# Two parts of the matmul array as neighbours: reordering the small products of an RWKV mixer

## The chip, the cores and the metric

The kernel runs on one core of a Trainium2 chip. That core has five engines with a queue each: TensorE (PE in the profile; its weight loads are PEld), VectorE (DVE), ScalarE (ACT), GpSimd (POOL) and SyncE (SP), which issues transfers here. Each engine takes its own instructions in order, and engines wait for each other through semaphores. Matmuls write to PSUM, which has eight banks; a tile of the kernel with 512 f32 columns fills one.

The metric is device time in microseconds: the median of several executions of the kernel, as they were shown.

## The reference

The reference is a two-layer encoder trunk with 1024 positions of width 1024. Layer 0 mixes with two head groups side by side: RWKV-7 (8 heads of 64) and gated DeltaNet (4 heads of 128). Layer 1 mixes with chunked attention. Each layer then has a squared-ReLU MLP and a gated per-layer embedding. Only the RWKV group, and an inverse that both groups use, are touched:

```python
def rwkv7_group(...):
    ...
    w_log = -jax.nn.softplus(-(w0 + jnp.tanh(xw @ w1) @ w2)) - 0.5
    decay = jnp.exp(-jnp.exp(w_log))
    a = jax.nn.sigmoid(a0 + (xa @ a1) @ a2)
    ...
    y = wkv7_scan(rh, heads(decay), kh, vh, -kk, kk * ah)
    ...

def step(state, inp):                       # of wkv7_scan
    r_t, w_t, k_t, v_t, a_t, b_t = inp
    sa = jnp.einsum('bhij,bhj->bhi', state, a_t)
    state = state * w_t[:, :, None, :] + sa[..., None] * b_t[:, :, None, :] + v_t[..., None] * k_t[:, :, None, :]
    return state, jnp.einsum('bhij,bhj->bhi', state, r_t)
```

The kernel does not step through positions. It works in chunks of 128 positions: within a chunk the recurrence is a unit lower triangular system, whose matrix is N, and whose inverse is formed once for each chunk and head. The state is carried from chunk to chunk.

## The kernel before

**Units and lanes.** Layer 0's mixer is cut into 16 units: for each half of the sequence (512 positions, four chunks of 128), four RWKV pairs of heads and four DeltaNet heads, alternating. A unit goes through five lanes, each a Python generator: `in` (projections), `front` (decay, N and its scores, the start of the inverse), `mid` (the end of the inverse), `back` (the recurrence over four chunks) and `post` (group norm and gate). `run` (L123) plays the lanes against a clock of its own: each matmul adds a modelled time to `self.now` (`mm`, L151), and each `yield` of a name holds a lane back for the time that the table `LAT` has for it, while other lanes go on. This sets the program order. When the context is closed, a scheduler that simulates the program (L1950) may still move an instruction ahead of others that are not ready. The projections are dense 128 x 128 x 512 products (tile `dps`) in a two-pass type (hi and lo parts); they fill the time in which other lanes wait.

**Banks.** Two of the eight PSUM banks hold the dense products. Six have one tag each: `tp` (front), `iz` (inverse), `pm` (masked scores), `ch` (steps of the recurrence), `y` (its output) and `pp` (post lane, `post_bank`, L520).

**An f32 product** appears in the trace as two passes, each a weight load and a matmul, so counts of the profile are twice the number of products. A shape such as 64*128 in a row of PE is the part of the array: 64 rows (the contraction) by 128 columns (the output's partitions).

**Low-rank products** (`rwkv_front`, L758). `lwa` holds, in partitions 0 to 63, the decay's low-rank input and, in 64 to 127, that of a. psw (L781) multiplies the upper half with `wa2`, psa (L807) the lower half; both go through `ptile`, bank `tp`, and both are read by a tanh on ACT (L783 and L809). Between them lies the work on the decay and a pause, `rwkv_front0` (L804).

**N scores** (L833 to L840). For each head h of the pair, rows 64h to 64h + 63: four 64 x 128 x 128 products, one for each chunk, into one bank `tp`; then four scaled evacuations on ACT into N; then a pause, `rwkv_front3`. So head 1 starts after head 0's pause.

**The inverse** (`inverse_end`, L393). N's diagonal blocks of 16 are inverted on POOL beforehand; then blocks are joined to 32, 64 and 128 for N = 8 (RWKV: four chunks of two heads) or 4 (DeltaNet: four chunks) matrices at once. Steps 0 and 1 join to 32, with products that go round all four 32-row groups. Steps 2 and 3 (tiles `T32`, `Z`, `X32`) join to 64: for each of two blocks, i = 0 and i = 2, all N products of 32 x 32 x 32 follow each other, first those of i = 0. Steps 5 and 6 (tile `TZ`, L455 and L460) join to 128: N products of 64 x 64 x 64 follow each other in one part of the array, their results lie in one half of the partitions, and one ACT copy takes them out.

**The recurrence** (`rwkv_back`, L871), for each of four chunks c: pw (inverse's right side), a copy W on ACT, pu = X W, scaled to U on DVE, then pu2, the state update, with one 128 x 64 x 64 product of Ktm and Vt and one of Btm and U for each head; S2 on DVE; the scores of the next chunk; and y: one 128 x 128 x 128 product of the state Sf with AR, and for each head one of Vt and one of U with masked scores `pmq`, which land in that head's half of the partitions. pw reads `pmq` of both heads.

Of the kernel before, what the change touches and what calls it, by code (L numbers as in the profile page):

```python
# [11 lines left out]
AF = mybir.ActivationFunctionType  # L12
# [5 lines left out]
P = 128  # L18
# [5 lines left out]
C = 128  # L24
# [80 lines left out]
class Trunk:  # L105
# [45 lines left out]
    def mm(self, out, lhsT, rhs, start, stop):  # L151
        n, m = 1, 1
        for c in rhs.shape[1:]:
            n *= c
        for c in lhsT.shape[1:]:
            m *= c
        if rhs.dtype == F32:
            self.now += 2 * max(n / 1200, m * 0.0007)
        else:
            self.now += max(n / 2400, m * 0.00035)  # L160
        return self.nc.tensor.matmul(out, lhsT, rhs, start=start, stop=stop)  # L161

    def tr(self, out, in_, ident):
        self.now += 0.107
# [228 lines left out]
    def inverse_end(self, Xp, B, N, F):  # L393

        nc, h2 = self.nc, self.mid
        V, A, G = nc.vector, nc.scalar, nc.gpsimd
        cur, curT = Xp[:, :, 0:16], Xp[:, :, 16:32]
        m1, m2 = self.half[:, 0:1], self.half[:, 1:2]
        quad = [slice(32 * i, 32 * i + 32) for i in range(4)]
        up, lo = slice(0, 64), slice(64, 128)  # L400

        def bank(w):
            return self.psm.tile([P, N, w], F32, tag="iz", name="iz")

# [24 lines left out]
        Z = T2  # L429
        for i in (0, 2):  # L430
            for g in range(N):
                self.mm(pz[quad[i + 1], g, :], B[quad[i], g, quad[i + 1]], T2[quad[i], g, :], start=True, stop=True)
        for i, cp in ((0, A.copy), (2, V.tensor_copy)):
            cp(Z[quad[i + 1]], pz[quad[i + 1]])
        for i in range(4):
            G.tensor_copy(F[quad[i], :, quad[i]], X2[quad[i]])
        yield f"inverse{N}_2"
        px = bank(32)
        for i in (0, 2):
            for g in range(N):  # L440
                self.mm(px[quad[i], g, :], Z[quad[i + 1], g, :], X2[quad[i + 1], g, :], start=True, stop=True)
        for i, cp in ((0, A.copy), (2, V.tensor_copy)):
            cp(F[quad[i], :, quad[i + 1]], px[quad[i]])
        yield f"inverse{N}_3"

        pt = bank(64)
# [7 lines left out]
        for g in range(N):  # L454
            self.mm(pz[lo, g, :], B[up, g, lo], TZ[up, g, :], start=True, stop=True)  # L455
        A.copy(TZ[lo], pz[lo])
        yield f"inverse{N}_5"
        px = bank(64)
        for g in range(N):
            self.mm(px[up, g, :], TZ[lo, g, :], F[lo, g, lo], start=True, stop=True)  # L460
        A.copy(F[up, :, lo], px[up])
        yield f"inverse{N}_6"


# [293 lines left out]
    def rwkv_front(self, p, hf, sc, raws, u):  # L758
        nc, h2, fr, sm, psm = self.nc, self.h2, self.fr, self.sm, self.psm
        V, A, G = nc.vector, nc.scalar, nc.gpsimd  # L760
        t2 = self.t2
# [9 lines left out]
        def ptile():  # L771
            return psm.tile([P, HB], F32, tag="tp", name="tp")
# [4 lines left out]
        sq = t2()  # L777
        A.activation(sq, kkr, AF.Square)

        psw = ptile()  # L780
        self.mm(psw, self.wa2[0:64, p * P:(p + 1) * P], sc["lwa"][0:64], start=True, stop=True)  # L781
        lw = t2()
        A.activation(lw, psw, AF.Tanh, bias=self.dv["hw0"][:, p:p + 1], scale=0.5)  # L783
        V.tensor_scalar(lw, lw, -0.5 * EXPM05, -0.5 * EXPM05, op0=ALU.mult, op1=ALU.add)
# [16 lines left out]
        A.activation(E, L, AF.Exp)  # L801
        Em = t2([P, 4, C])
        A.activation(Em, L[:, :, 1:C + 1], AF.Exp, scale=-1.0)
        yield "rwkv_front0"  # L804

        psa = ptile()
        self.mm(psa, self.wa2[64:128, p * P:(p + 1) * P], sc["lwa"][64:128], start=True, stop=True)  # L807
        ta = t2()
        A.activation(ta, psa, AF.Tanh, bias=self.dv["ha0"][:, p:p + 1], scale=0.5)  # L809
        yield "rwkv_front1"  # L810
        pst = ptile()
        for c in range(4):
# [1 line left out]
        cc = sm.tile([P, 8], F32, tag="cc", name="cc", bufs=4)  # L814
# [9 lines left out]
        Bt, Kt = t2(tag="b"), t2(tag="b")  # L824
# [5 lines left out]
            yield ("mid", u - 2)  # L830

        N = self.mid.tile([P, 8, P], F32, tag="n8", name="N")
        for h in range(2):  # L833
            sl = slice(64 * h, 64 * h + 64)
            ps = ptile()
            for c in range(4):
                self.mm(ps[:, c * C:(c + 1) * C], Bt[sl, c * C:(c + 1) * C], AR[sl, c, 0, :], start=True, stop=True)
            for c in range(4):
                A.activation(N[:, 4 * h + c, :], ps[:, c * C:(c + 1) * C], AF.Copy, scale=cc[:, 2 * c + h:2 * c + h + 1])
# [31 lines left out]
    def rwkv_back(self, p, hf, sc, st, u):  # L871
# [35 lines left out]
        for c in range(4):  # L907
# [36 lines left out]
            for h in range(2):  # L944
# [1009 lines left out]
```

## Time and profile before

| | |
|---|---|
| median of three runs | 3194.34 us (3192.11 to 3196.0) |
| the profiled execution | 3200.01 us, span 3198.3 us |
| mean granted clock of TensorE | 0.974 |
| PE in 0 to 110 us | 91.33 us busy |
| PE in 945 to 970 us (the last head of layer 0) | 18.76 us busy |
| PE in 970 to 1750 us (layer 0's MLP and what follows) | 780.00 us busy |
| PE in 1750 to 2395 us (layer 1's attention) | 590.80 us busy |
| PE in 2395 to 3198.3 us (layer 1's MLP and what follows) | 798.18 us busy |

The profile is of one execution. A row of its groups names the line, the engine, the operation and the tiles (out<-in), the part of the array, the shape and the count, then busy time, the mean of one, and the idle time ahead of it. As every matmul is recorded by one helper, they all have line L161 (transposes L165) and are told apart by their tiles: `tp<-lao,wa` are the low-rank products, `tp<-AR,b` the N scores, `iz<-T,N`, `iz<-X,T`, `iz<-TZ,N` and `iz<-F,TZ` the inverse (with Ng in place of N for DeltaNet), `ch<-b,tm` and `ch<-U,tm` the state update, `py<-...` the output y. A row of the timeline begins with the start and the length in us and ends with the count of passes in it. Matmuls are pipelined, so lengths overlap.

### The profile page before, as it was taken

To read this page: it belongs to the slowest core of one execution; us is meant where nothing else is said; L and a number is where in the kernel's file an instruction comes from. 1 tells how busy PE (TensorE), PEld (TensorE's weight loads), DVE (VectorE), ACT (ScalarE), POOL (GpSimd) and SP (SyncE) were. 2 spreads that over 40 slices of the span, in tenths; PEclk is the share of its full clock that TensorE was granted. 3 is DMA by queue.
4 is the path that set the end of the run, shared out by engine and by line. 5 is a ranking of instruction groups with operands and counts; after the bars stand their busy time and mean duration, and the time that the engine had idled before them with its cause. 6 is when DMAs were issued, how large, how long until landed. Compare 5 with 4: busy or idle time off the path is not lost.

```text
span 3198.3 us, 46044 instructions
## 1 busy us (share of the span) xinstructions
PE 3102.1 (97%) x17576; PEld 2565.6 (80%) x17576; DVE 2013.2 (63%) x4020; ACT 1384.2 (43%) x2608; POOL 531.5 (17%) x978
## 2 busy tenths in 40 slices
PE   7999999999999999999999898999899999999999
PEld 5777777777777888888888888988778888888887
DVE  6566675556748666655546576776768666655552
ACT  4333333334326555322123477777756555312121
POOL 6334442433410000000004211010110000000002
PEclk8999899999899999999999999999999999999999
DMA  3322112212325433523213210110156433522213
GB/s 120 94 63 60 47 46 67 70 61 70 129 95 194 155 119 108 192 93 106 92 51 128 70 36 32 45 41 16 69 177 209 150 121 109 185 105 92 106 47 105
DMA packets 144716, 309.60 MB, mean 97 GB/s; under 512 B 40944, under 2 KB 43120, under 8 KB 144496
## 3 DMA queue, kind: packets, MB, share of 16 engines
q1 hardware_dynamic: 126064, 273.10, 25.6%
q10 hardware_dynamic: 18432, 33.56, 2.7%
q8 instruction: 138, 2.26, 0.3%
q14 instruction: 82, 0.67, 0.1%
HBM read 232.16 MB, written 74.45 MB: 96 GB/s over the span
## 4 chain that ended last, share of the span: by engine, by line
PE 85%; DVE 7%; ACT 3%; DMA 2%; issue 1%; POOL 0%; SPq 0%; ACTq 0%; DVEq 0%; POOLq 0%
PE dps L161 70%; PE ch L161 3%; PE iz L161 2%; PE pm L161 2%; PE tp L161 1%; PE po L161 1%; PE py L161 1%; DVE ptile L318 1%; PE pt L165 1%; DMA wraw<-in_w_qkv 1%; PE sn L161 1%; PE pp L161 1%; DVE pb L1795 1%; PE sc L161 1%; ACT pb L1808 1%
## 5 line engine op out<-in xcount | busy, mean ns | idle before, releaser
L161 PE MATMUL dps<-r,act 128*128 128x512 f32 x3528 | 824.4, 392 | 0.0
L161 PEld LDWEIGHTS dps<-r,act 128*128 128x128 f32 x3528 | 662.1, 188 | 145.7
L161 PE MATMUL dps<-xg,whi 128*128 128x512 f32 x1280 | 438.2, 418 | 11.7 <-ACT xg L320 7.3
L161 PE MATMUL dps<-late,act 128*128 128x512 f32 x1536 | 352.9, 391 | 0.0
L161 PEld LDWEIGHTS dps<-late,act 128*128 128x128 f32 x1536 | 288.4, 188 | 63.1
L161 PE MATMUL dps<-wq,act 128*128 128x384 f32 x1536 | 304.8, 344 | 5.8 <-DVE vs L1704 3.1
L1452 POOL TENSOR_TENSOR pn<-pn,prs 128x512 f32<-128x512 f32 x32 | 45.5, 1426 | 1590.7 <-ACT prs L354 1496.3
L161 PEld LDWEIGHTS dps<-xg,whi 128*128 128x128 f32 x1280 | 248.4, 199 | 75.2 <-issue 10.7
L161 PEld LDWEIGHTS dps<-wq,act 128*128 128x128 f32 x1536 | 265.6, 191 | 10.4 <-DVE vs L1704 5.1
L161 PE MATMUL dps<-xg,wlo 128*128 128x512 f32 x640 | 266.4, 416 | 3.1 <-DVE wlo L277 3.1
L1328 DVE TENSOR_TENSOR late<-late,dps 128x512 f32<-128x512 f32 x224 | 152.9, 685 | 150.1 <-PE dps L161 119.2
L1427 DVE TENSOR_TENSOR xw<-xw,dps 128x512 f32<-128x512 f32 x192 | 131.5, 685 | 148.4 <-PE dps L161 145.5
L1226 ACT CAST act<-act 128x1024 fp32r<-128x1024 f32 (+1 forms) x99 | 94.8, 964 | 285.2 <-DMA act<-in_w 124.2
L1226 ACT CAST act<-late 128x512 fp32r<-128x512 f32 x210 | 124.5, 618 | 135.9 <-PE dps L161 117.0
L1227 DVE TENSOR_TENSOR act<-late,act 128x512 fp32r<-128x512 f32 x210 | 139.9, 687 | 26.1 <-ACT act L1226 25.9
L161 PEld LDWEIGHTS dps<-xg,wlo 128*128 128x128 f32 x640 | 126.9, 198 | 34.1 <-issue 4.8
L161 PE MATMUL dps<-xw,act 128*128 128x512 f32 x576 | 138.9, 392 | 0.0
L276 ACT CAST whi<-wraw 128x1024 fp32r<-128x1024 f32 x78 | 81.7, 1047 | 124.2 <-PE dps L161 74.4
L161 PEld LDWEIGHTS dps<-xw,act 128*128 128x128 f32 x576 | 108.1, 188 | 24.1
L1227 DVE TENSOR_TENSOR act<-act 128x1024 fp32r<-128x1024 f32 (+1 forms) x99 | 109.9, 1115 | 21.0 <-ACT act L1226 19.8
L161 PE MATMUL po<-ptile,vs 128*128 128x256 f32 (+1 forms) x576 | 104.9, 297 | 17.1 <-DVE ptile L318 7.7
L277 DVE TENSOR_TENSOR wlo<-wraw,whi 128x1024 fp32r<-128x1024 f32 x78 | 101.4, 1301 | 25.6 <-ACT whi L276 25.6
(472 smaller groups left out, 5369.4 us busy)
## 6 DMA issues: line engine op xcount, KB each, us to landing
act<-in_w SPq DMA_DIRECT2D x68, 512.0 KB
hd<-late ACTq DMA_DIRECT2D x128, 256.0 KB
late<-in_w SPq DMA_DIRECT2D x60, 512.0 KB
wraw<-in_w_in SPq DMA_DIRECT2D x56, 512.0 KB
act<-hd SPq DMA_DIRECT2D x56, 512.0 KB
wraw<-in_w_out SPq DMA_DIRECT2D x21, 512.0 KB
wraw<-in_w_qkv SPq DMA_DIRECT2D x21, 512.0 KB
pn<-pnd SPq DMA_DIRECT2D x32, 256.0 KB
```

Of the source, the lines that this page charges most:

```text
L161: return self.nc.tensor.matmul(out, lhsT, rhs, start=start, stop=stop)
L165: return self.nc.tensor.transpose(out, in_, ident)
L276: nc.scalar.copy(hi, raw)
L277: nc.vector.tensor_tensor(lo, raw, hi.bitcast(F32), op=ALU.subtract)
L318: nc.vector.tensor_tensor(dst[:, 1, sl], src, dst[:, 0, sl].bitcast(F32), op=ALU.subtract)
L1226: A.copy(hi, s)
L1227: V.tensor_tensor(lo, s, hi.bitcast(F32), op=ALU.subtract)
L1328: V.tensor_tensor(r, t, u, op=ALU.add)
L1427: V.tensor_tensor(x[n][:, sl], x[n][:, sl], ps, op=ALU.add)
L1452: G.tensor_tensor(pn, pn, prs[:, sl], op=ALU.mult)
L1795: V.tensor_tensor_reduce(S, pn[:, 0:nn * P], toep[:, (3 - nn) * P:], op0=ALU.add, op1=ALU.max, scale=1.0, scalar=NEG, accum_out=mx[:, 0:1])
L1808: A.activation(S, S, AF.Exp, bias=mx[:, 2:3], accum_out=l[:, 0:1])
```

## The change

- A helper, `together`, adds edges without semaphores between the matmuls of a list, so that they keep that order.
- psw and psa are issued as neighbours, psa first, psa into the post lane's bank `pp`. Both tanh follow, that of psa first. The pause `rwkv_front0` goes.
- The N scores of the two heads alternate, chunk by chunk, into two banks (`tp` for head 0, `pp` for head 1); all eight evacuations follow, those of head 1 first. One pause `rwkv_front3` is left of two.
- In steps 2 and 3 of the inverse the loops over i and g are exchanged, so that products in different parts of the array alternate.
- In steps 5 and 6 the results of even g go to the upper half of the partitions and those of odd g to the lower; two ACT copies take them out.
- In the recurrence, the state's product for y is issued ahead of the pause `rwkv_back5`; the state update goes Ktm of both heads, then Btm of both heads; and the head products of y follow it in the same manner, Vt of both heads, then U of both heads, ahead of S2 and of the next scores.

The table `LAT` and the modelled times of `mm` are as before.

```diff
+    def together(self, products):
+
+        edge = mybir.DependencyInfo(mybir.DependencyClass.NoSync, mybir.DependencyReason.DATA)
+        for u, v in zip(products, products[1:]):
+            self.tc.add_manual_dep(v.ins, u.ins.name, edge, reason="together")
...
-        for i in (0, 2):
-            for g in range(N):
+        for g in range(N):
+            for i in (0, 2):
                 self.mm(pz[quad[i + 1], g, :], B[quad[i], g, quad[i + 1]], T2[quad[i], g, :], start=True, stop=True)
...
+        part = lambda t, e: t[:, e::2, :]
+
+        def both(ps, f):
+            for g in range(N):
+                f(ps[up if g % 2 == 0 else lo, g, :], g)
+
+        def out(dst, ps):
+            for e, r in ((0, up), (1, lo)):
+                A.copy(part(dst, e), part(ps[r], e))
...
-        for g in range(N):
-            self.mm(pz[lo, g, :], B[up, g, lo], TZ[up, g, :], start=True, stop=True)
-        A.copy(TZ[lo], pz[lo])
+        both(pz, lambda o, g: self.mm(o, B[up, g, lo], TZ[up, g, :], start=True, stop=True))
+        out(TZ[lo], pz)
...
-        psw = ptile()
-        self.mm(psw, self.wa2[0:64, p * P:(p + 1) * P], sc["lwa"][0:64], start=True, stop=True)
+        psw, psa = ptile(), self.post_bank()
+        self.together([self.mm(ps, self.wa2[r, p * P:(p + 1) * P], sc["lwa"][r], start=True, stop=True)
+                       for ps, r in ((psa, slice(64, 128)), (psw, slice(0, 64)))])
+
+        ta = t2()
+        A.activation(ta, psa, AF.Tanh, bias=self.dv["ha0"][:, p:p + 1], scale=0.5)
...
-        yield "rwkv_front0"
-
-        psa = ptile()
-        self.mm(psa, self.wa2[64:128, p * P:(p + 1) * P], sc["lwa"][64:128], start=True, stop=True)
-        ta = t2()
-        A.activation(ta, psa, AF.Tanh, bias=self.dv["ha0"][:, p:p + 1], scale=0.5)
         yield "rwkv_front1"
...
+        pn = [ptile(), self.post_bank()]
+        ms = []
+        for c in range(4):
+            for h in (1, 0):
+                sl = slice(64 * h, 64 * h + 64)
+                ms.append(self.mm(pn[h][:, c * C:(c + 1) * C], Bt[sl, c * C:(c + 1) * C], AR[sl, c, 0, :],
+                                  start=True, stop=True))
+        self.together(ms)
+        for h in (1, 0):
             for c in range(4):
-                self.mm(ps[:, c * C:(c + 1) * C], Bt[sl, c * C:(c + 1) * C], AR[sl, c, 0, :], start=True, stop=True)
-            for c in range(4):
-                A.activation(N[:, 4 * h + c, :], ps[:, c * C:(c + 1) * C], AF.Copy, scale=cc[:, 2 * c + h:2 * c + h + 1])
-            yield "rwkv_front3"
+                A.activation(N[:, 4 * h + c, :], pn[h][:, c * C:(c + 1) * C], AF.Copy, scale=cc[:, 2 * c + h:2 * c + h + 1])
+        yield "rwkv_front3"
...
+            py_c = py[:, c * C:(c + 1) * C]
+            self.mm(py_c, Sf, AR[:, c, 1, :], start=True, stop=False)
             yield "rwkv_back5"
+
             pu2 = psm.tile([P, HB], F32, tag="ch", name="ch")
-            for h in range(2):
-                self.mm(pu2[hs[h], 0:64], Ktm[:, c, hs[h]], Vt[:, c, hs[h]], start=True, stop=False)
-                self.mm(pu2[hs[h], 0:64], Btm[:, c, hs[h]], U[:, hs[h]], start=False, stop=True)
+            for t, v in ((Ktm, Vt[:, c]), (Btm, U)):
+                for h in range(2):
+                    self.mm(pu2[hs[h], 0:64], t[:, c, hs[h]], v[:, hs[h]], start=t is Ktm, stop=t is Btm)
+            for v, j in ((Vt[:, c], 2), (U, 0)):
+                for h in range(2):
+                    self.mm(py_c[hs[h]], v[:, hs[h]], pmq[c, h][:, j, :], start=False, stop=j == 0)
...
-            py_c = py[:, c * C:(c + 1) * C]
-            self.mm(py_c, Sf, AR[:, c, 1, :], start=True, stop=False)
-            for h in range(2):
-                self.mm(py_c[hs[h]], Vt[:, c, hs[h]], pmq[c, h][:, 2, :], start=False, stop=False)
-                self.mm(py_c[hs[h]], U[:, hs[h]], pmq[c, h][:, 0, :], start=False, stop=True)
             yield "rwkv_back6"
```

More of the change, by code (lines that the diff above doesn't have):

```diff
@@ L438, in inverse_end @@
         px = bank(32)
-        for i in (0, 2):
-            for g in range(N):
+        for g in range(N):
+            for i in (0, 2):
                 self.mm(px[quad[i], g, :], Z[quad[i + 1], g, :], X2[quad[i + 1], g, :], start=True, stop=True)
@@ L444, in inverse_end @@
         yield f"inverse{N}_3"
+        part = lambda t, e: t[:, e::2, :]
+        def both(ps, f):
+            for g in range(N):
+                f(ps[up if g % 2 == 0 else lo, g, :], g)
+        def out(dst, ps):
+            for e, r in ((0, up), (1, lo)):
+                A.copy(part(dst, e), part(ps[r], e))
         pt = bank(64)
@@ L453, in inverse_end @@
         pz = bank(64)
-        for g in range(N):
-            self.mm(pz[lo, g, :], B[up, g, lo], TZ[up, g, :], start=True, stop=True)
-        A.copy(TZ[lo], pz[lo])
+        both(pz, lambda o, g: self.mm(o, B[up, g, lo], TZ[up, g, :], start=True, stop=True))
+        out(TZ[lo], pz)
         yield f"inverse{N}_5"
         px = bank(64)
-        for g in range(N):
-            self.mm(px[up, g, :], TZ[lo, g, :], F[lo, g, lo], start=True, stop=True)
-        A.copy(F[up, :, lo], px[up])
+        both(px, lambda o, g: self.mm(o, TZ[lo, g, :], F[lo, g, lo], start=True, stop=True))
+        out(F[up, :, lo], px)
         yield f"inverse{N}_6"
@@ L832, in rwkv_front @@
         N = self.mid.tile([P, 8, P], F32, tag="n8", name="N")
-        for h in range(2):
-            sl = slice(64 * h, 64 * h + 64)
-            ps = ptile()
+        pn = [ptile(), self.post_bank()]
[7 more added lines that the diff above has]
+        for h in (1, 0):
             for c in range(4):
-                self.mm(ps[:, c * C:(c + 1) * C], Bt[sl, c * C:(c + 1) * C], AR[sl, c, 0, :], start=True, stop=True)
-            for c in range(4):
-                A.activation(N[:, 4 * h + c, :], ps[:, c * C:(c + 1) * C], AF.Copy, scale=cc[:, 2 * c + h:2 * c + h + 1])
-            yield "rwkv_front3"
+                A.activation(N[:, 4 * h + c, :], pn[h][:, c * C:(c + 1) * C], AF.Copy, scale=cc[:, 2 * c + h:2 * c + h + 1])
+        yield "rwkv_front3"
         X = self.inverse_start(N, 8)
@@ L941, in rwkv_back @@
                 scores(c + 1, 1)
-            py_c = py[:, c * C:(c + 1) * C]
-            self.mm(py_c, Sf, AR[:, c, 1, :], start=True, stop=False)
-            for h in range(2):
-                self.mm(py_c[hs[h]], Vt[:, c, hs[h]], pmq[c, h][:, 2, :], start=False, stop=False)
-                self.mm(py_c[hs[h]], U[:, hs[h]], pmq[c, h][:, 0, :], start=False, stop=True)
             yield "rwkv_back6"
```

## The prediction

> **What bounds the kernel now.** I read four views in this order: the page, a table by stretches, the waits of the matmul engine, and then its timeline around each product that the diff moves. First the page:
>
> ```profile
> span 3198.3 us, 46044 instructions
> ...
> PE 3102.1 (97%) x17576; PEld 2565.6 (80%) x17576; DVE 2013.2 (63%) x4020; ACT 1384.2 (43%) x2608; POOL 531.5 (17%) x978
> ...
> PE 85%; DVE 7%; ACT 3%; DMA 2%; issue 1%; POOL 0%; SPq 0%; ACTq 0%; DVEq 0%; POOLq 0%
> ```
>
> The chain that ends last runs through PE. The edits lie in layer 0's mixer, so the question is whether PE is the limit there. The stretches, and PE's waits between 110 and 945 us:
>
> ```profile
> 110.00:945.00 835.00, 823.00 (x6642) 643.75 (x6641) 519.36 (x1189) 308.96 (x622) 318.44 (x703) 0.95 0.23 72
> ...
> PE ch L161 <- ACT W L920: 3.4, 1, 3.4
> ```
>
> The columns are the length, then the busy time of PE, PEld, DVE, ACT and POOL, then the granted clock. From 110 to 945 us PE is idle for 835.00 - 823.00 = 12 us, and its longest wait is 3.4 us. All other engines have room. So in this stretch a microsecond of PE work that goes away should come off the end, until the waits that PE's work covers today come out.
>
> A busy PE is not a full one. An f32 product appears in the trace as two passes, each with its own weight load, and a pass on a part of the array leaves the rest free. What counts is the distance from one start to the next, so I read starts below, not durations.
>
> **Do two parts of the array run at once here?** This decides the sign, and the trace of before has cases by chance. Rows apart, with 64-row tiles into two banks:
>
> ```profile
> 516.67 0.92 PE L161 MATMUL pm<-AR,b 64*128 64x128 f32 x4
> 517.52 0.49 PE L161 MATMUL py<-AR,Sh 128*128 128x128 f32 x2
> 517.94 0.43 PE L161 MATMUL py<-PMQ,b 128*64 128x128 f32 x2
> 518.30 0.50 PE L161 MATMUL iz<-TZ,Ng 64*64 64x64 f32 x5
> ...
> 576.52 0.68 PE L161 MATMUL iz<-F,TZ 64*64 64x64 f32 x8
> 577.13 0.69 PE L161 MATMUL tp<-lao,wa 64*128 64x512 f32 x1
> 577.13 0.70 PE L161 MATMUL pm<-AR,b 64*128 64x128 f32 x3
> ...
> 577.68 0.38 PE L161 MATMUL pm<-AR,b 64*128 64x256 f32 x1
> 578.18 0.50 PE L161 MATMUL dps<-xg,whi 128*128 128x512 f32 x1
> ```
>
> Alone, the four pm passes take 517.52 - 516.67 = 0.85 us. Beside a low-rank product both together take 578.18 - 577.13 = 1.05 us, which is what that product takes alone (below). The second comes free. Columns apart, with the same 128 rows:
>
> ```profile
> 526.12 0.34 PE L161 MATMUL ch<-b,tm 128*64 128x64 f32 x4
> 526.29 0.29 PE L161 MATMUL ch<-U,tm 128*64 128x64 f32 x4
> 526.40 0.28 PE L161 MATMUL py<-PMQ,U 128*64 128x128 f32 x1
> 526.42 0.28 PE L161 MATMUL py<-PMQ,b 128*64 128x128 f32 x1
> ...
> 526.64 0.38 PE L161 MATMUL py<-PMQ,U 128*64 128x128 f32 x2
> 526.95 0.50 PE L161 MATMUL dps<-xg,whi 128*128 128x512 f32 x1
> ```
>
> The eight 64-column passes of the state update take 526.40 - 526.12 = 0.28 us; one after another at 0.058 us each (worked out below) they would take 0.46 us. And U of one head and Vt ("b") of the other start 0.01 to 0.02 us apart. The text has each head's two products behind each other, so neighbours up to about four passes away find each other already.
>
> **The change part by part**, in PE time, for 8 rwkv and 8 gdn units.
>
> *Low-rank products.* psw and psa are two visits of PE today; `together` makes psw follow psa, in the other rows and in another bank.
>
> ```profile
> 457.23 0.39 PE L161 MATMUL dps<-xg,whi 128*128 128x512 f32 x1
> 457.55 1.12 PE L161 MATMUL tp<-lao,wa 64*128 64x512 f32 x2
> 458.60 0.50 PE L161 MATMUL dps<-xg,whi 128*128 128x512 f32 x1
> ...
> 478.76 1.16 PE L161 MATMUL tp<-AR,b 64*128 64x128 f32 x8
> 479.85 0.37 PE L161 MATMUL iz<-T,Ng 32*32 32x16 f32 x22
> ```
>
> A product takes 458.60 - 457.55 = 1.05 us. Eight pairs save 8 x 1.05 = 8.4 us if each was alone. Some were not, as at 577 us; I allow for two or three, and take 6. Bounds: 0 (the pair is torn apart) and 9.
>
> *N scores.* Four products of one head take 479.85 - 478.76 = 1.09 us; both heads then fit in the time of one: 8 x 1.09 = 8.7, and the entry of one visit less (457.55 - 457.23 = 0.32 us for a dense pass ahead of a visit) gives a little more: 9. Bounds 0 and 9.6.
>
> *Steps 2 and 3 of the inverse.* Products of 32 x 32 now alternate between two tiles that share neither rows nor columns.
>
> ```profile
> 450.57 0.69 PE L161 MATMUL iz<-X,T 32*32 32x32 f32 x16
> 451.19 0.66 PE L165 MATMUL tp<-ident,f 128*128 128x128 f32 x4
> ...
> 695.02 0.59 PE L161 MATMUL iz<-T,Ng 32*32 32x32 f32 x16
> 695.54 0.50 PE L161 MATMUL dps<-xg,whi 128*128 128x512 f32 x1
> ...
> 877.20 1.09 PE L161 MATMUL iz<-T,N 32*32 32x32 f32 x32
> 878.23 0.48 PE L161 MATMUL pm<-AR,b 64*128 64x128 f32 x2
> ```
>
> 32 passes take 1.03 us, 16 of one tile 0.62: as pairs the 32 need about 0.62, so 16 visits of rwkv save 16 x 0.41 = 6.6. A gdn visit takes 0.52 and would fall to about 0.36: 16 x 0.15 = 2.4. Sum 9, bounds 0 and 12.
>
> *Steps 5 and 6.* 64 x 64 products alternate between two column halves of the same rows.
>
> ```profile
> 466.91 1.14 PE L161 MATMUL iz<-TZ,N 64*64 64x64 f32 x16
> 467.99 0.50 PE L161 MATMUL dps<-xg,wlo 128*128 128x512 f32 x1
> ...
> 618.88 0.44 PE L161 MATMUL iz<-TZ,Ng 64*64 64x64 f32 x4
> 619.25 0.34 PE L161 MATMUL ch<-b,tm 128*64 128x64 f32 x4
> ```
>
> 16 passes take 1.08 us, 8 (at 576.52) 0.61, 4 take 0.37; a pass costs (1.08 - 0.61) / 8 = 0.058 us. As pairs 16 cost what 8 do, and 8 what 4 do: 16 x 0.47 + 16 x 0.24 = 11. The price is a second evacuation on ACT, since the results lie in two partition halves:
>
> ```profile
> L456 ACT COPY TZ<-iz 64x512 f32<-64x512 f32 x8 | 4.7, 582 | 5.7 <-PE iz L161 5.6
> L456 ACT COPY TZ<-iz 64x256 f32<-64x256 f32 x8 | 2.9, 367 | 17.3 <-PE iz L161 17.2
> L839 ACT ACTIVATE N<-tp,cc 128x128 f32<-128x128 f32 x56 | 16.0, 368 | 23.2 <-PE tp L161 23.2
> ```
>
> One copy of 512 columns (0.58 us) becomes two of 256 (0.73), so each of 32 stages is ready some 0.15 us later: 5 us if nothing covered it. Dense passes of the projections lie in these gaps, so I charge half. Bounds of the part: 6 and 11.
>
> *State update and y.* The state update's passes overlap already (0.28 us above): nothing. For y, Vt of head 0 is issued early today, alone, for 518.30 - 517.94 = 0.36 us; U of head 0 pairs with Vt of head 1, and U of head 1 runs alone: 526.95 - 526.40 = 0.55 us. In the new order both Vt are neighbours. Both are ready where the early one goes, since the step before them reads the masked scores of both heads; so the second comes free there, and both U pair at about 0.33 us. That saves 0.22 us in each of 32 chunks: 7. Moving Sf x AR ahead changes little: the trace has it two stages early already (517.52). Bounds: -4 (Vt of head 1 alone, a visit more at 0.36 less what it relieves) and 12 (all four in one visit, 0.38 us a chunk).
>
> *Front lane.* Two planned pauses go. Both heads' eight evacuations of N (0.368 us each) now stand in one row on ACT, 2.9 us instead of twice 1.5; a copy of W behind them comes later. psa and one head's scores go to the bank of the post lane. I count this into the waits.
>
> The sum is 6 + 9 + 9 + 11 + 7 = 42 us of PE time. To be given back: 2.5 us for the second copies, and 3.5 us for waits whose cover got thinner (today 12 us of idle time). Net 36, with 0 to 26 given back as bounds. The profiled execution took 3200.01 us (span 3198.3), 5.7 us more than the median 3194.34. So 3200.0 - 36 = 3164, and for the median **3158 us**.
>
> **A rule that speaks against it.** The trace's row for column halves is the 0.28 us at 526.12. The Trainium skill, page "TensorE: Matmul & The Clock Gate", section "The mechanism", says that a weight load overlaps running matmuls only where the row groups differ. Steps 5 and 6 and y share their rows. By that rule they would gain nothing; the trace disagrees, since eight loads and passes on the same 128 rows took 0.28 us.
>
> **Rivals.**
> 1. *The waits come out.* PE reaches waiting instructions early. The 16 units have some 7 inverse stages and 12 steps of the recurrence each, about 300 waits; at 0.07 us each 21 us return besides the second copies. Against it: PE waits only 12 us today. 3200 - 42 + 23.5 = 3181.5, median 3176. Chance 16%.
> 2. *Column halves do not overlap in weight loads.* Steps 5, 6 and y fall out: 24 - 6 = 18 us, median 3176. Against it stands 526.12. Chance 3%.
> 3. *The neighbours are torn apart.* The edges order the products but do not glue them; another ready instruction gets between. Then only the inverse gains, 20 - 6 = 14 us: median 3180. The runs of 8, 16 and 32 passes quoted above speak against it. Chance 8%.
> 4. *Slower: the post lane's bank.* psa and one head's scores need the bank "pp", which the post lane holds while DVE catches up. PE takes its queue in order, so each of the 16 new takers that waits for the bank stops all dense work behind it. At 36 / 16 = 2.25 us each the gain is gone; at 3.5 us the time is 3200 - 36 + 56 = 3220, median 3214. Against it: the longest of the bank's five readers is short, and there are seven of it in this stretch:
>
> ```profile
> L981 DVE SCALAR_TENSOR_TENSOR o<-o,vecs,pp 128x512 f32<-128x512 f32 x7 | 5.2, 746 | 4.1 <-PE pp L161 4.0
> ```
>
> Chance 7%.
>
> **How the numbers follow.** The forecast has 66%; alone it spans 3146 (all upper bounds, 54 us, with the median's offset 3140) to 3170. Rivals 1 to 3 reach up to 3180. A further unknown is the clock, which stands at half in some stretches:
>
> ```profile
> 831.50:848.60 17.10, 16.59 (x83) 13.24 (x84) 15.56 (x36) 8.18 (x15) 11.92 (x24) 0.50 0.53 159
> ```
>
> Here PE is busy at a granted 0.50. If all that is missing from the mean of 0.95 in 110 to 945 us is of this kind, it is 2 x 0.05 x 835 = 84 us; one stretch like this more or less moves the time by up to 8 us. So the range is 3140 to 3184. A measurement of this kernel tells about 0.2% (6 us) from no change. Faster by more: forecast, rivals 1 to 3 nearly whole, 0.88; within: 0.05; slower: 0.07.
>
> **What would show it.** Right: the low-rank passes as four at once in about 1.05 us; 16 N passes in about 1.1; 32-pass visits of steps 2 and 3 near 0.62; 16-pass visits of steps 5 and 6 near 0.61; y's early visit still about 0.36 with both heads; PE still idle under 20 us between 110 us and the end of the mixer, and the MLP's start 36 us earlier. Wrong: pairs with other work between them; waits of PE on ACT's TZ, F or W copies or on readers of pp; more stretches at half clock.

## The result and the profile after

The changed kernel takes 3202.02 us, the median of 17 executions (3191.88 to 3209.53); the kernel before, on the same chip, 3196.0 us (17 executions). The ratio is 1.0018, 95% interval 1.0007 to 1.0028. The 36 us that were forecast did not come; the time is outside the range. The profiled execution took 3205.34 us.

The page of the changed kernel, with the span, the busy times and the chain that ended last:

```profile
span 3203.6 us, 46065 instructions
...
PE 3088.4 (96%) x17576; PEld 2551.5 (80%) x17576; DVE 2003.8 (63%) x4020; ACT 1388.0 (43%) x2640; POOL 529.4 (17%) x978
...
PE 86%; DVE 7%; ACT 3%; DMA 2%; issue 1%; POOL 1%; SPq 0%; DVEq 0%; ACTq 0%; POOLq 0%
```

The span is 5 us longer, yet PE is busy for 14 us less: even the busy time hardly fell, for 42 us of work that should have gone. The table by stretches shows why. Changed kernel first, up to 945 us and then up to the end of its mixer:

```profile
110.00:945.00 835.00, 810.80 (x6593) 629.04 (x6592) 513.07 (x1183) 311.17 (x647) 316.83 (x702) 0.90 0.23 72
77.00:978.80 901.80, 867.67 (x6870) 673.75 (x6868) 537.09 (x1245) 325.19 (x675) 331.70 (x740) 0.90 0.23 73
```

The same view of the kernel before, up to the end of its mixer:

```profile
77.00:969.40 892.40, 874.16 (x6867) 683.47 (x6865) 543.08 (x1243) 321.73 (x644) 331.45 (x740) 0.94 0.23 73
```

After the length and the five busy times (PE, PEld, DVE, ACT, POOL) stands the granted clock. Between 77 us and the end of the mixer PE is idle for 901.80 - 867.67 = 34 us (before: 18), and its clock is 0.90 instead of 0.94. The trace's clock records, of which these are rounded means, know two levels only, 1.0 and 0.5: before, PE ran at half clock for 104 us in 14 stretches, now for 185 us in 21. (From here on "idle" and "half clock" always run from 77 us to the end of the mixer, the first dense product after the last transpose of the post lane.) That is one execution of each; the others agree. The mean granted clock of a whole execution was 0.959 to 0.967 in the 17 of the changed kernel, and 0.969 to 0.977 in those of the kernel before that ran beside the experiments.

So the end of the mixer can be split: end = work + idle + half clock / 2, where work is what PE would need at full clock, with the first 77 us counted whole.

| | mixer ends | idle | half clock | work at full clock |
|---|---|---|---|---|
| before | 969.4 | 18.2 | 103.9 | 899.2 |
| changed | 978.8 | 34.2 | 185.0 | 852.1 |

**The forecast saving came, 47 us of work for 42 predicted. 16 us came back as idle time and 40.5 us as half clock.** The split is rough in two ways. Idle time inside half clock (8.9 us before, 10.9 now) counts in both columns, and the first 77 us hold idle time and half clock of their own (18.7 and 16.9 us before, 21.7 and 19.7 now). Split from 0 us on, 51 us of work went, and 19 and 42 us came back. What follows the mixer takes 2225 us against 2229: nothing of it lies there.

Seven of the eight low-rank pairs and all eight visits of N scores stand as described. The timeline of PE in the changed kernel, at the low-rank pair, at the N scores, and at steps 3, 5 and 6 of the inverse:

```profile
498.14 0.69 PE L161 MATMUL pp<-lao,wa 64*128 64x512 f32 x1
498.15 0.69 PE L161 MATMUL tp<-lao,wa 64*128 64x512 f32 x1
498.67 0.59 PE L161 MATMUL pp<-lao,wa 64*128 64x512 f32 x1
498.68 0.59 PE L161 MATMUL tp<-lao,wa 64*128 64x512 f32 x1
499.20 0.44 PE L161 MATMUL py<-PMQ,b 128*64 128x128 f32 x4
...
514.43 0.37 PE L161 MATMUL pp<-AR,b 64*128 64x128 f32 x1
514.44 0.37 PE L161 MATMUL tp<-AR,b 64*128 64x128 f32 x1
...
515.53 0.44 PE L161 MATMUL py<-PMQ,b 128*64 128x128 f32 x4
...
684.90 0.69 PE L161 MATMUL iz<-X,T 32*32 32x32 f32 x32
685.52 0.66 PE L161 MATMUL ch<-b,PMQ 128*128 128x64 f32 x4
...
699.34 0.68 PE L161 MATMUL iz<-TZ,N 64*64 64x64 f32 x16
699.95 0.51 PE L161 MATMUL dps<-xg,whi 128*128 128x512 f32 x1
```

From start to start: both low-rank products 499.20 - 498.14 = 1.06 us (predicted 1.05), both heads' N scores 515.53 - 514.43 = 1.10 (about 1.1), 32 passes of 32 x 32 in 0.62 (0.62), 16 of 64 x 64 in 0.61 (0.61), y's early visit with both heads 0.37 (0.36).

One low-rank pair is torn apart. psa of the second RWKV unit goes out alone, and its psw follows 80 us later:

```profile
74.75 2.07 PE L161 MATMUL pp<-lao,wa 64*128 64x512 f32 x2 [3.62 <-ACT N L855]
...
154.79 1.12 PE L161 MATMUL tp<-lao,wa 64*128 64x512 f32 x2
```

Now two places where the time went. The timeline of PE in the changed kernel:

```profile
388.42 0.36 PE L161 MATMUL iz<-Xp,Z 32*32 32x16 f32 x18
390.96 0.37 PE L161 MATMUL pp<-AR,b 64*128 64x128 f32 x1 [2.18 <-DVE b L837]
...
839.14 0.66 PE L161 MATMUL ch<-b,PMQ 128*128 128x64 f32 x4
839.64 1.00 PE L161 MATMUL dps<-ones,xg 128*128 128x1 f32 x8
840.57 0.92 PE L161 MATMUL pm<-AR,b 64*128 64x128 f32 x4
841.42 0.49 PE L161 MATMUL ch<-Sh,AR 128*128 128x128 f32 x2
```

and its stretches around them:

```profile
388.40:391.80 3.40, 1.22 (x33) 1.10 (x34) 3.40 (x5) 1.16 (x3) 3.15 (x4) 1.00 0.01 2
391.80:398.60 6.80, 6.80 (x36) 5.23 (x34) 3.27 (x7) 2.17 (x8) 2.25 (x5) 0.50 0.23 82
...
839.00:842.40 3.40, 3.29 (x25) 2.65 (x24) 3.40 (x10) 3.37 (x9) 2.81 (x7) 1.00 0.93 289
842.40:859.50 17.10, 15.85 (x64) 12.75 (x63) 16.14 (x39) 9.01 (x16) 14.60 (x23) 0.50 0.41 129
```

The first: N's pair waits 2.18 us for DVE, and the 6.8 us after it run at 0.50, which costs 3.4 more. The second: PE is busy for 3.29 of 3.40 us and waits for next to nothing, and 17.1 us at half clock follow. In that window PE ran sums on one column, products on half of the array and a few on all of it with 64 or 128 columns, and no dense product. The half-clock stretches last 3.4, 6.8, 10.2, 13.7 or 17.1 us: whole numbers of 3.41 us. So in these traces the clock changes window by window, and being busy is not enough to keep it.

### The profile page after: what moved, and what is told of

The parts are those of the page before. It is cut to its first block, busy times and chain, and to the rows that moved or that the text cites. A ratio compares the mean times of both kernels' runs of the same rounds, so it can differ in the third digit from the quotient of the medians.

```text
span 3203.6 us, 46065 instructions
## 1 busy us (share of the span) xinstructions
PE 3088.4 (96%) x17576; PEld 2551.5 (80%) x17576; DVE 2003.8 (63%) x4020; ACT 1388.0 (43%) x2640; POOL 529.4 (17%) x978
## 4 chain that ended last, share of the span: by engine, by line
PE 86%; DVE 7%; ACT 3%; DMA 2%; issue 1%; POOL 1%; SPq 0%; DVEq 0%; ACTq 0%; POOLq 0%
PE dps L161 72%; PE ch L161 2%; PE pm L161 2%; PE iz L161 1%; PE po L161 1%; PE pp L161 1%; PE pt L171 1%; DVE ptile L324 1%; PE py L161 1%; PE sn L161 1%; DMA wraw<-in_w_qkv 1%; DVE pb L1812 1%; ACT pb L1825 1%; PE tp L161 1%; PE sc L161 0%
## 5 line engine op out<-in xcount | busy, mean ns | idle before, releaser
L161 PE MATMUL dps<-xg,whi 128*128 128x512 f32 x1280 | 446.7, 426 | 19.1 <-ACT xg L326 7.7
L161 PEld LDWEIGHTS dps<-xg,whi 128*128 128x128 f32 x1280 | 252.7, 202 | 82.0 <-issue 10.2
```

## The experiments

All but one are timed in three rounds, 4 to 10 executions, against the kernel before on the same chip, which read 3195.0 to 3199.0 us. Differences between two experiments are good to some 4 us, since they come from different chips. The columns of the tables: median, ratio with 95% interval, then idle, half clock and work as above. These last three are of one profiled execution of each, which can lie 8 us above the median (`wide_nolora`, `wide2_a`).

**The parts alone** (each is the kernel before with one part; `front_only` is the low-rank pair, the N pairs and both pauses gone).

`inv_only` has the edits of steps 2, 3, 5 and 6 of the inverse, and `back_only` those of the recurrence, as the diff of the change has them:

```diff
-        for i in (0, 2):
-            for g in range(N):
+        for g in range(N):
+            for i in (0, 2):
```

```diff
+            for v, j in ((Vt[:, c], 2), (U, 0)):
+                for h in range(2):
+                    self.mm(py_c[hs[h]], v[:, hs[h]], pmq[c, h][:, j, :], start=False, stop=j == 0)
```

`no_pauses` leaves every product as before:

```diff
-        yield "rwkv_front0"
...
-            yield "rwkv_front3"
+        yield "rwkv_front3"
```

> Only steps 2, 3, 5 and 6 of the inverse are changed (pairs of tiles, two copies); both pauses, the front lane and the recurrence are as before. Theory A (thin cover): the faster products leave stretches with little array work, the clock falls to half more often, and the part gives back what it saves: 3190 to 3200 us, more than 150 us at half clock in the mixer (126 before, 208 after the whole change). Theory B (moved dense passes): the pairs by themselves gain, and the loss comes from the pauses taken out of the front lane's plan: about 3178 us (20 us of products less 2.5 for the copies), half clock near 126 us.

> Only the recurrence is changed (order of state update and y). Theory A: 3190 to 3200 us, more time at half clock than 126 us. Theory B: about 3188 us (7 us saved), half clock near 126 us.

> Only the front lane is changed: low-rank pair, N pairs, second bank, and both pauses gone. Theory A: 3190 to 3200 us. Theory B: the loss sits here: 15 us saved, but slower than before in total, 3200 to 3220 us, with most of the added half clock (200 us).

> Nothing of the products is changed; only the two planned pauses of the front lane (rwkv_front0 and the one between the two heads' N scores) are taken out. Theory A: no change, 3190 to 3198 us, since no product got faster. Theory B: slower by 20 us or more, 3215 us or above, with PE waits and half clock grown.

`lora_only` has the low-rank pair alone (its bank and its pause with it), `n_only` the N pairs alone (second bank, one pause):

> The kernel before with the low-rank pair alone (psa in the post lane's bank, one pause gone). Prediction's term: 6 us less PE work. If the time went to the clock: work at full clock falls by 4 to 8 us, half clock and idle time rise, and the time stays within 6 us of the kernel before. If the post lane's bank stalls PE: waits on readers of pp of a microsecond and more, and the kernel is slower by over 6 us.

> The kernel before with the N pairs alone (second bank, one pause gone). Prediction's term: 9 us less PE work. If the thinner cover of N's evacuations on ACT matters: idle time of PE at products that read N or need the bank, and more half clock than 104 us, so that 0 to 5 us of the 9 remain at most. If the bank stalls PE: waits of over 1 us before the N products in most of the eight units, and slower by over 6 us.

| | median | ratio | idle | half clock | work |
|---|---|---|---|---|---|
| inv_only | 3199.64 | 1.0008 (0.9996 to 1.0019) | 24.3 | 123.6 | 885.1 |
| back_only | 3206.63 | 1.0032 (1.0018 to 1.0046) | 28.5 | 116.1 | 889.1 |
| front_only | 3206.75 | 1.0034 (1.0015 to 1.0053) | 21.1 | 155.7 | 884.7 |
| no_pauses | 3198.65 | 1.0003 (0.9991 to 1.0014) | 21.4 | 106.1 | 899.1 |
| lora_only | 3203.69 | 1.0026 (1.0013 to 1.0038) | 23.4 | 131.2 | 887.2 |
| n_only | 3190.82 | 0.9978 (0.9961 to 0.9995) | 23.6 | 106.9 | 887.2 |

(The 126 and 208 us of half clock in the first expectation are counted from 0 to 980 us; from 77 us to the end of the mixer they are 104 and 185.) Each part takes 10 to 14 us of work away, and only one, N, makes the kernel faster. The other parts pay it back, as 12 to 52 us more at half clock (half of it counts) and 3 to 10 us of idle time. Removing the pauses alone does nothing. Neither theory fits all four: `inv_only` has the time of theory A without its 150 us of half clock, and `back_only` is slower than both. The low-rank pair, with 7.5 us lost, lies 1.5 us beyond what its expectation allowed. The bank does not stop PE: its longest wait ahead of a product into `pp` is 1.2 us, for the post lane's own input on ACT (the kernel before has the same wait). That the bank makes a front lane later is not excluded by this. The stretches of `lora_only` and then of `n_only`:

```profile
77.00:976.20 899.20, 875.84 (x6858) 687.36 (x6856) 536.09 (x1243) 321.36 (x641) 331.52 (x740) 0.93 0.23 73
```

```profile
77.00:964.20 887.20, 863.60 (x6850) 673.54 (x6849) 532.48 (x1243) 320.84 (x640) 335.11 (x740) 0.94 0.24 74
```

**The pauses put back** into the changed kernel:

```diff
+        yield "rwkv_front0"
         yield "rwkv_front1"
...
-        yield "rwkv_front3"
+            yield "rwkv_front3"
```

> The changed kernel with both planned pauses put back (one ahead of the low-rank pair's readers, one behind each head's N evacuations). If the pauses were the cause of the loss: 3190 or less, idle time back towards 20 us. If the loss comes from thin cover and the clock, as the run with only the pauses gone says: within 8 us of the changed kernel's 3202, with over 150 us at half clock.

3196.61 us, ratio 1.0000 (0.9987 to 1.0014): 5 us less than the changed kernel, with 170 us at half clock and 40 idle. The pauses are not the cause of the main loss.

**The plan's prices.** `honest` is the changed kernel, where the modelled time of the paired products in `mm` is halved, as the trace has it, so that the plan of lanes knows of the pairs:

```diff
-    def mm(self, out, lhsT, rhs, start, stop):
-        n, m = 1, 1
+    def mm(self, out, lhsT, rhs, start, stop, par=1):
+        n, m, now = 1, 1, self.now
...
+        self.now = now + (self.now - now) / par
```

> The changed kernel, with one thing more: the plan's modelled time of every product that now has a partner in another part of the array is halved (steps 2, 3, 5, 6, low-rank, N scores, state update and head products of y), so the program order lays out more dense passes behind them. No product changes. If the loss comes from a plan that counts the pairs at their old price: PE's idle time falls from 34 to about 20 us, half clock from 185 to 130 us or less, 3165 to 3185 us. If the loss has nothing to do with the plan: 3195 to 3207 us, as the changed kernel.

3181.93 us, ratio 0.9949 (0.9929 to 0.9969), with idle 36.8, half clock 149.5, work 852.3. With the work unchanged, the end moves by the half clock that the other order has less (35 us, half of it counts). The time is the one expected of a cause in the plan, but idle time did not fall to 20 us, nor half clock to 130.

**Feeding the clock.** In the kernel before and the changed one, sums over partitions are products on one or two columns: norms in RWKV's front and post lanes and in DeltaNet's. Here 64 columns take their place (32 equal ones for each head in RWKV, 64 equal ones in DeltaNet); one of the equal results is read:

```diff
-            self.mm(pst[:, 2 * c:2 * c + 2], sq[:, c * C:(c + 1) * C], self.hsel, start=True, stop=True)
+            self.mm(pst[:, 64 * c:64 * c + 64], sq[:, c * C:(c + 1) * C], self.blk[:, 32:96], start=True, stop=True)
...
-        V.tensor_scalar(cc, pst[:, 0:8], 1e-6, None, op0=ALU.add)
+        V.tensor_scalar(cc, pst[:, 0:256:32], 1e-6, None, op0=ALU.add)
```

`wide_b` has this on the kernel before, `wide_a` on the changed one, `honest_wide` on `honest`; `wide2_a` has besides X W on 128 columns instead of 64, half of it unread.

> The kernel before, with the products of 1 or 2 columns (sums of squares of both groups, front and post lanes) given 64 equal columns; their passes are bound by the weight load (0.112 us), so they take the same time, but more of the array works. If the clock falls where a window of 3.4 us has little array work, whatever PE's busy time: half clock falls from 104 us to under 70, and the time to 3180 us or less. If it falls where PE waits: no change, 3192 to 3200 us, 104 us of half clock.

> The same on the changed kernel. Array work decides: half clock falls from 185 to under 130 us, 3175 to 3190 us. PE's waits decide: 3198 to 3207 us, half clock as in the changed kernel.

> Both: the plan with halved prices and the wide sums. If both causes are real: 3160 us or less, half clock under 90 us. If only one is, as that one's kernel alone.

> The changed kernel with its sum products on 64 equal columns, and besides that X x W of the recurrence on all 128 columns of W instead of one head's 64 (half of the result isn't read): 128 passes more array work for nothing. If the clock goes by array work: under 100 us at half clock up to the end of the mixer (104 without the edit, 185 in the changed kernel) and a time of 3172 or less. If what counts is PE's busy time or its idle time alone: no less half clock than without the edit, and 3172 or more by what the longer passes cost (up to 128 x 0.03 = 4 us).

| | median | ratio | idle | half clock | work |
|---|---|---|---|---|---|
| wide_b | 3188.38 | 0.9969 (0.9955 to 0.9983) | 23.8 | 69.8 | 905.1 |
| wide_a | 3172.62 | 0.9907 (0.9878 to 0.9936) | 37.0 | 104.4 | 856.7 |
| honest_wide | 3176.81 | 0.9925 (0.9899 to 0.9951) | 45.5 | 107.6 | 853.3 |
| wide2_a | 3168.85 | 0.9917 (0.9889 to 0.9945) | 33.4 | 109.8 | 859.6 |

Work that nobody reads makes the changed kernel 29 us faster. Its half clock falls from 185 to 104 us, to what it was before the change, at an idle time that did not fall. `wide_b` reached the half clock that was expected, but not the time (3188 us, expected 3180 or less). The stretches of `wide_a` up to 945 us, beside the changed kernel's 0.90:

```profile
110.00:945.00 835.00, 798.96 (x6719) 619.49 (x6718) 530.47 (x1226) 313.66 (x660) 321.19 (x702) 0.94 0.24 74
```

Once this is done, the plan's better prices add nothing, against the expectation of `honest_wide`. The wider X W is not settled. Its profiled execution, the slowest of four, has no less half clock than `wide_a` (110 us), but the mean granted clock of its four executions is 0.973 to 0.981, that of `wide_a` 0.972 to 0.975, and the two medians are 4 us apart. The rule had to be measured by itself.

**The clock by itself.** `clock_probe`, run once, is the kernel before with rows of products behind its last work, which nothing reads; PE is never idle in them:

```diff
+        kinds = [(full, 1, 100), (full, 16, 100), (full, 32, 100), (full, 48, 100), (full, 64, 100),
+                 ((h[0], [h[0]]), 64, 180), ((h[0], h), 64, 360), ((slice(0, 32), [slice(0, 32)]), 32, 260)]
+        for (rows, cols), n, count in kinds:
+            for (r, cs), m, k in ((full, HB, 20), ((rows, cols), n, count)):
+                for q in range(k):
+                    c = cs[q % len(cs)]
+                    o = 0 if m == HB else q % 8 * 64
+                    v = self.mm(ps[c, o:o + m], self.ident[r, c], x[r, 0:m], start=True, stop=True)
```

> The kernel before with rows of f32 products behind its last work; nothing of them is stored. Eight kinds of 100 to 360 products each, and ahead of each kind 20 products of the full array on 512 columns, which bring the clock back: full weights on 1, 16, 32, 48 and 64 columns, one 64 x 64 tile on 64 columns, 64 x 64 tiles that alternate between two column halves, and one 32 x 32 tile on 32 columns. PE is busy throughout. If the clock goes by array work (columns x 0.83 ns x share of the array, bound at about 1.2 us in 3.41 us; a full pass up to 64 columns starts every 0.112 us, a 64 x 64 one every 0.058): half clock for 1 (0.03 us), 16 (0.4), 32 (0.8) columns, the single 64 x 64 tile (0.8) and the 32 x 32 tile (0.1); full clock for 64 columns (1.6) and the two column halves (1.6); 48 (1.2) is on the edge. If it goes by PE's busy or idle time: full clock throughout.

The stretches of `clock_probe`: products of the full array on 512 columns, then one row for each kind in that order, without its first windows:

```profile
3191.00:3207.00 16.00, 16.00 (x38) 7.03 (x37) 0.00 (x0) 0.00 (x0) 0.00 (x0) 1.00 0.04 16
...
3213.00:3245.00 32.00, 32.00 (x151) 32.00 (x152) 0.00 (x0) 0.00 (x0) 0.00 (x0) 0.50 0.00 1
3268.00:3305.00 37.00, 37.00 (x175) 37.00 (x175) 0.00 (x0) 0.00 (x0) 0.00 (x0) 0.50 0.00 0
3329.00:3362.00 33.00, 33.00 (x157) 33.00 (x156) 0.00 (x0) 0.00 (x0) 0.00 (x0) 0.50 0.00 0
3387.00:3419.00 32.00, 32.00 (x152) 32.00 (x152) 0.00 (x0) 0.00 (x0) 0.00 (x0) 0.50 0.00 1
3440.00:3461.00 21.00, 21.00 (x191) 21.00 (x189) 0.00 (x0) 0.00 (x0) 0.00 (x0) 1.00 0.01 2
3479.00:3499.00 20.00, 20.00 (x346) 20.00 (x345) 0.00 (x0) 0.00 (x0) 0.00 (x0) 1.00 0.01 2
3518.00:3538.00 20.00, 20.00 (x694) 20.00 (x691) 0.00 (x0) 0.00 (x0) 0.00 (x0) 1.00 0.02 5
3561.00:3577.00 16.00, 16.00 (x307) 16.00 (x304) 0.00 (x0) 0.00 (x0) 0.00 (x0) 0.50 0.02 3
```

PE is busy for 100% in all rows, and the clock is 0.50 in five of the eight kinds. With the full array a pass on 1, 16, 32 or 48 columns is held at half clock, 32 / 151 = 0.21 us each; on 64 columns it keeps full clock, 21 / 191 = 0.11 us each. So, in a long row of such passes, 64 columns take half of the time that one column takes. One of eight went against the expectation: a single 64 x 64 tile on 64 columns stays at full clock, though by share of the array (0.8 us of work in 3.41) it should have lost it. The Trainium skill, page "TensorE: Matmul & The Clock Gate", section "What's actually happening", says that a monitor looks at windows of 3413 ns and sets the clock by how busy PE was. The window agrees (all half-clock lengths above are multiples of 3.41 us). "Busy" as the profile counts it does not: PE was busy for 100% in the rows at 0.50.

**What to leave out.** From the kernel with wide sums, one edit of the change taken back each: the recurrence's order (`wide_noback`), the low-rank pair (`wide_nolora`), the pauses (`wide_pauses`, the diff above), and pair and order (`wide_nl_nb`). `after_nolora` takes the pair out of the changed kernel itself, and with it the second bank, the missing pause and the order of the two tanh; the sums are as they were:

```diff
-        psw, psa = ptile(), self.post_bank()
-        self.together([self.mm(ps, self.wa2[r, p * P:(p + 1) * P], sc["lwa"][r], start=True, stop=True)
-                       for ps, r in ((psa, slice(64, 128)), (psw, slice(0, 64)))])
...
+        psw = ptile()
+        self.mm(psw, self.wa2[0:64, p * P:(p + 1) * P], sc["lwa"][0:64], start=True, stop=True)
...
+        yield "rwkv_front0"
+
+        psa = ptile()
+        self.mm(psa, self.wa2[64:128, p * P:(p + 1) * P], sc["lwa"][64:128], start=True, stop=True)
```

> The changed kernel with sum products on 64 columns and the recurrence's order of the kernel before. If the new order of y gains nothing because it gives its 10 us back as idle time: 3172 within 5, idle time some 8 us less than the 37 with it. If it gains its term of 7 once the clock is fed: 3177 or more.

> The changed kernel with sum products on 64 columns and the two low-rank products as before (apart, own bank, pause between). If the pair costs more than it gains (it was 7 us slower alone): 3168 or less. If its loss alone was the clock: 3175 to 3179, its term of 6 us lost.

> The changed kernel with sum products on 64 columns and both pauses put back. With 1-column sums the pauses brought 5 us (3196.6 against 3202). If that was by the clock (170 us at half clock against 185): 3170 to 3175, no gain beside the wide sums. If the pauses help by themselves: 3168 or less.

> The changed kernel with the two low-rank products as before (apart, own bank, pause between), the sum products on 1 and 2 columns. If the pair costs by itself, as beside the wide sums (3172.6 with it, 3154.6 without): 3188 or less, idle time 8 us under the changed kernel's 34. If it cost only through the wide sums' timing: 3200 to 3210, its term of 6 us lost.

> The changed kernel with sum products on 64 columns, and both the low-rank pair and the recurrence's new order as before: what stays is the inverse, N and the wide sums. If the two losses (18 and 6 us) are of separate places: 3149 or less. If both are the same loss, cover that stands too thin in one stretch: 3155 or more.

| | median | ratio | idle | half clock | work |
|---|---|---|---|---|---|
| wide_noback | 3166.06 | 0.9897 (0.9882 to 0.9912) | 33.6 | 95.7 | 865.4 |
| wide_nolora | 3154.55 | 0.9859 (0.9842 to 0.9875) | 25.0 | 86.2 | 860.7 |
| wide_pauses | 3189.17 | 0.9969 (0.9954 to 0.9984) | 43.5 | 124.2 | 853.4 |
| after_nolora | 3166.26 | 0.9914 (0.9893 to 0.9935) | 34.3 | 97.7 | 857.4 |
| wide_nl_nb | 3157.02 | 0.9883 (0.9866 to 0.9899) | 30.9 | 63.0 | 867.5 |

The stretches of `after_nolora`, up to the end of its mixer at 940.5 us:

```profile
77.00:940.50 863.50, 829.26 (x6852) 645.67 (x6850) 537.95 (x1242) 326.31 (x672) 339.76 (x740) 0.94 0.24 76
```

**The low-rank pair costs the changed kernel its gain.** Without it the time is 3166.26 us: 36 us less than with it (33 by the two ratios), 0.9914 of the kernel before. Idle time is the same (863.50 - 829.26 = 34 us, not 8 less, as was expected; in the first 77 us it is 4 us less), work is 5 us more, the pair's saving (11 when split from 0 us on); but half clock falls from 185 to 98 us, worth 44 us. The mean granted clock was 0.974 or 0.975 in all four executions, against 0.959 to 0.967 with the pair. The recurrence's order saves its work too (6.8 to 8.7 us here, 7 predicted) and gives it back: the mixers of `wide_a` and `wide_noback` end at 945.9 and 946.8 us, and by the medians the new order costs 7 us (3 by the ratios), which neither branch of its expectation had. The losses of pair and order do not add up (`wide_nl_nb` is no faster than `wide_nolora`). The pauses, which helped by 5 us beside the narrow sums, cost 17 us beside the wide ones. So they seem to act through the order that the plan makes with them; the expectation missed it. The fastest kernel is `wide_nolora`: 0.9859 (0.9842 to 0.9875) of the kernel before.

## Why the prediction was wrong, point by point

- **What bounds the kernel.** Right that PE bounds this stretch. Too short: "a microsecond of PE work that goes away should come off the end" counts PE's work at one clock, and the clock changed with what stood in a window: wider sums alone, which nobody reads, took 81 us of half clock away.
- **The terms of the sum** were about right: 47 us for 42 in total. Alone, the inverse took 14 us of work away (20), the recurrence 10 (7), N 12 (9), the low-rank pair 12 alone and 5 to 11 in the changed kernel (6).
- **Column halves with the same rows** run side by side, 16 passes in 0.61 us, so rival 2 fell. The Trainium skill, page "TensorE: Matmul & The Clock Gate", section "The mechanism", has a weight load overlap only where row groups differ; these runs disagree.
- **Given back in waits, a term sized too small:** 3.5 us predicted, 16 us measured, so most of rival 1's 21 came. They are spread: 2.18 us for N at 390.96 is one of the longest. Taken alone, each part adds 3 to 10 us. (The upper end of the forecast's own span, 3170, is worked out from none of its terms; with the 26 us that it allows to be given back it would be 3178.)
- **The clock, the step that failed.** "One stretch like this more or less moves the time by up to 8 us" was a spread around a mean. It was seven stretches and 81 us more at half clock: 40.5 us, all to one side. The sign that the prediction named for this, more stretches at half clock, came. The dense products are as many as before but stand less evenly: of the 3.41 us windows from 77 us to the end of the mixer, 35 of 261 held no dense pass (none of 512 columns on all rows began in them) before, 47 of 263 after the change, 38 of 252 without the low-rank pair. The 17.10 us row at 0.50 with PE busy for 16.59, which the prediction quotes, already said that busy time does not keep the clock.
- **Rival 3** fell in the main: all N visits and seven of eight low-rank pairs are whole; the second unit's is torn, in every run with the pair. **Rival 4** fell in the form that it was given, with PE stopped at each taker: PE waits ahead of a low-rank pair for the bank's reader, ACT's N, once, for the 3.6 us at 74.75 us, as the row of groups by form of the changed kernel says:

```profile
L161 PE MATMUL pp<-lao,wa 64*128 64x512 f32 x16 | 9.9, 703 | 3.6 <-ACT N L855 3.6
```

- **What stays open.** That the pair's loss is half clock is shown; why one visit of 1.05 us instead of two makes that difference is not. The pauses alone do not. The bank, which no run changes alone, may do it without stopping PE: in all ten runs with the pair, psw of the third RWKV unit starts at 273 to 286 us (changed kernel: 278.0, behind the post lane's last reader of `pp` at 275.7), in the nine without it at 244 to 253. Whether the loss follows from this later front lane is not shown. Putting work elsewhere changes the order that the plan and the scheduler choose for the whole mixer, and several runs (pauses, prices) moved 5 to 20 us by order alone. A part's price in one order is not its price in another: the pair loses 7 us alone, 36 in the changed kernel, 18 beside wide sums (by the medians).

## What to carry to other kernels

Where the trace shows stretches at half clock, split a stage into work at full clock, idle time and half clock before summing savings: a saving of PE work can be paid back twice, by waits and by windows at half clock. Look at those windows for products on few columns, and try widening them to 64 columns where a pass takes no longer for it (here about 0.11 us at full clock for 64 columns, and as much for one: eight passes from 839.64 to 840.57 us). Then try each part of a bundled change by leaving it out of the whole, since alone it may show the other sign.

## What was not expected of the hardware

- With the full array PE keeps its clock from 64 columns a pass on and loses it at 48, though it is busy for 100% in both. A 64 x 64 tile on 64 columns keeps it, a 32 x 32 tile on 32 columns loses it. Counting 0.82 ns a column (16.00 / 38 / 512 us), times the share of rows in use, over the time from pass to pass at full clock, gives 0.36 for 48 columns (0.11 us), 0.45 for the 64 x 64 tile (20 / 346 = 0.058 us), 0.48 for 64 columns: a bound between 0.36 and 0.45 would fit all eight kinds. That is an estimate. By share of the whole array the 64 x 64 tile, which keeps its clock, would stand at 0.23, under the 48 columns that lose it. In the 231 windows of the kernel before that begin at full clock, though, the best bound by share of rows (0.375) puts 6 on the wrong side and one by share of the whole array 4, so that the weighting stays open.
- Wide sums cost the kernel some 6 us of work (905.1 against 899.2), and win 17 us in half clock there (104 to 70) and 40 in the changed kernel.
